# Seven block products in place of eight in a streaming-encoder block, with weight tiles of four k-tiles

## Chip, core and metric

The kernel runs on one NeuronCore of a Trainium2 chip. The metric is the device time of one execution in microseconds (us); less is better. The five engines have a queue of instructions each and wait for one another through semaphores: TensorE (PE in the rows; its weight loads are PEld), VectorE (DVE), ScalarE (ACT), GpSimd (POOL) and SyncE (SP), which issues the DMA loads here.

## What is computed

One layer in float32 on 256 tokens of width 2048:

```
h = x + 1/2 * swiglu(rms_norm(x), ffn1 weights)        # 2048 -> 5632 -> 2048
u = rms_norm(h); proj = u @ w_in; pooling branch and chunked attention branch
gates = sigmoid(u @ w_branch_gate + b)
h = h + (g_pool * (y_pool @ w_br_pool) + g_attn * (y_attn @ w_br_attn)) @ w_out
h = h + 1/2 * swiglu(rms_norm(h), ffn2 weights)
h = h + sigmoid(rms_norm(h) @ w_ple_gate) * (p @ w_ple)

def swiglu(x, w_gate, w_up, w_down):
    return (jax.nn.silu(x @ w_gate) * (x @ w_up)) @ w_down
```

All weights, some 400 MB, are read from HBM once.

## The kernel before

Every large product is made in three float32r matmuls: a float32 x is split into hi, a ScalarE cast to float32r, and lo = x - hi, a VectorE subtraction (`split`, L107 to L109), and a @ w becomes lo·hi + hi·hi + hi·lo, all into one accumulator (L153 to L155). Tokens lie in two tiles of 128 (`NT`), output columns in blocks of 512 (`NB`, a PSUM bank), K in tiles of 128.

`product` (L134) makes one block of 512 columns for both token tiles. A weight tile of two k-tiles (`KW`, 512 KB) is loaded into one of six buffers `wraw`, and split into `whi` and `wlo`, three buffers each (`weight`, L127). The split of the next tile is written ahead of this tile's 12 matmuls. The activation operand (`u`, or `hid` for the hidden columns) is split and turned to [k, token] once: a finished piece is transposed on TensorE some weight tiles later (`later`, `step`), so that TensorE does not wait for it.

A feed-forward network (`ffn`, L274) runs in three parts of 4, 4 and 3 blocks of hidden columns: for each block the gate product, then the up product, silu(gate) x up (`hb`, L290), and after a part the down products, added to `h` at L299. The 11 blocks of the two networks, the mixing stage between them and the last gate (`ple`, L542) all use `product`.

TensorE's instructions stand in the order written; those of the other engines are ordered by a scheduler once the first weight tiles are through (`ORDERED`). Buffers of a pool are taken in turn: the next tile of a name waits until the oldest one's last reader is done.

Of the kernel before, what the change touches and what calls it, by code (L numbers as in the profile page):

```python
# [16 lines left out]
P = 128  # L17
# [11 lines left out]
REACH = 16  # no window is longer  # L29
ORDERED = 5  # weight tiles until the scheduler orders the other engines  # L30
EPS = 1e-6
MASK_VALUE = -1e30
NB = 512  # output columns of one accumulator (a PSUM bank)
KB = 4  # k-tiles of one activation tile
KW = 2  # k-tiles of one weight tile
FFN_PARTS = (4, 4, 3)  # blocks of NB hidden columns between two down projections


@with_exitstack
def hybrid_block(ctx: ExitStack, tc: tile.TileContext, a: dict, out: bass.AP):  # L40
# [6 lines left out]
    ps_acc = ctx.enter_context(tc.tile_pool(name="ps_acc", bufs=5, space=bass.MemoryType.PSUM))  # L47
    ps_tp = ctx.enter_context(tc.tile_pool(name="ps_tp", bufs=3, space=bass.MemoryType.PSUM))
# [9 lines left out]
    # Vectors that are needed with their channel on the partitions: rows of 128, turned at once.  # L58
# [22 lines left out]
    def col(name, i=0, n=1):  # L81
        return cols[name][:, i:i + n]

# [1 line left out]
    # TensorE takes its instructions in the order written here. What turns a product's result is  # L85
    # written some weight tiles later, so that it never waits for the engines before it.
    waiting = []
    steps = [0]
    order = ExitStack()  # of the first weight tiles, where the loads of x and theirs take turns
# [16 lines left out]
    # hi keeps 12 significant bits, lo = x - hi the other 12: x == hi + lo.  # L106
# [4 lines left out]
    newest = [None]  # the weights' last load  # L111

    def load(w, kt, n0):
        raw = wpool.tile([P, KW, NB], F32, tag="wraw", name="wraw", bufs=6)
        newest[0] = nc.sync.dma_start(
            raw, w[kt * P:(kt + KW) * P, n0:n0 + NB].rearrange("(k p) n -> p k n", p=P)
        )
# [7 lines left out]
    loaded = []  # of the first product: loads that run between those of x  # L125

    def weight(w, kt, n0):  # L127
        raw = loaded.pop(0) if loaded else load(w, kt, n0)
        hi = wpool.tile([P, KW, NB], F32R, tag="whi", name="whi", bufs=3)
        lo = wpool.tile([P, KW, NB], F32R, tag="wlo", name="wlo", bufs=3)  # L130
        split(hi, lo, raw)
        return hi, lo

    def product(w, lhs, n0, k0=0):  # L134
        """[token, NB] accumulators of lhs @ w[k0*P:, n0:n0+NB]; lhs: Operands of up to KB k-tiles."""
        acc = [ps_acc.tile([P, NB], F32, tag="acc", name="acc") for _ in range(NT)]
        nk = sum(o.hi.shape[1] for o in lhs)
        ahead = weight(w, k0, n0)
        for kt in range(0, nk, KW):
            step()  # L140
            whi, wlo = ahead
            if kt + KW < nk:
                ahead = weight(w, k0 + kt + KW, n0)
            for o in {lhs[(kt + k) // KB] for k in range(KW)}:
                while o.missing:
                    step()
            for t in range(NT):
                tt = slice(t * P, (t + 1) * P)
                for k in range(KW):
                    o, kk = lhs[(kt + k) // KB], (kt + k) % KB  # L150
                    xh, xl = o.hi[:, kk, tt], o.lo[:, kk, tt]
                    first, last = kt + k == 0, kt + k == nk - 1
                    nc.tensor.matmul(acc[t], xl, whi[:, k, :], start=first, stop=False)  # L153
                    nc.tensor.matmul(acc[t], xh, whi[:, k, :], start=False, stop=False)  # L154
                    nc.tensor.matmul(acc[t], xh, wlo[:, k, :], start=False, stop=last)  # L155
        return acc

    class Operand:
        def __init__(self, pool, tag, bufs, nk=KB, missing=NT):
            self.hi = pool.tile([P, nk, SEQ], F32R, tag=tag + "hi", name=tag + "hi", bufs=bufs)  # L160
            self.lo = pool.tile([P, nk, SEQ], F32R, tag=tag + "lo", name=tag + "lo", bufs=bufs)
            self.missing = missing

    def turn(dst, src, t):
        """Columns of src [token, NB] become the k-tiles of dst at tokens of tile t."""
        tp = ps_tp.tile([P, NB], F32, tag="tp", name="tp")
        for j in range(KB):
            nc.tensor.transpose(tp[:, j * P:(j + 1) * P], src[:, j * P:(j + 1) * P], ident)  # L168
        tpv = tp.rearrange("p (j s) -> p j s", j=KB)
        tt = slice(t * P, (t + 1) * P)  # L170
        split(dst.hi[:, :, tt], dst.lo[:, :, tt], tpv)
        dst.missing -= 1

    def turn_gain(dst, srcs, ts, gain):
        """The same for h * gain, at the tokens of several tiles."""
        gained = []
        for src in srcs:
            tp = ps_tp.tile([P, NB], F32, tag="tp", name="tp")
            for j in range(KB):
                nc.tensor.transpose(tp[:, j * P:(j + 1) * P], src[:, j * P:(j + 1) * P], ident)  # L180
            g = work.tile([P, KB, P], F32, tag="gained", name="gained", bufs=2)
            nc.vector.tensor_tensor(  # L182
                out=g, in0=tp.rearrange("p (j s) -> p j s", j=KB),
                in1=gain.unsqueeze(2).to_broadcast([P, KB, P]), op=ALU.mult,
            )
            gained.append(g)
        for t, g in zip(ts, gained):
            tt = slice(t * P, (t + 1) * P)
            split(dst.hi[:, :, tt], dst.lo[:, :, tt], g)
            dst.missing -= 1  # L190

# [1 line left out]
    def rsqrt_mean(ssq, n, count, name, bufs):  # L193
# [6 lines left out]
        # One step of Newton takes the table's error out.  # L200
# [7 lines left out]

    class Norm:
# [3 lines left out]
        def __init__(self, gain):  # L213
            self.gain = gain
            self.ssq = work.tile([P, NT, D // NB], F32, tag="ssq", name="ssq", bufs=2)
            self.u = []

        def open(self, b):
            self.u.append(Operand(act, "u", D // NB))

        def turn(self, b, ts):
# [390 lines left out]
```

## Time and profile before

| what | value |
|---|---|
| median of 3 runs | 2147.14 us (2147.13 to 2147.52) |
| span of the profiled execution | 2146.3 us |
| PE busy | 2136.9 us (100%) |
| DVE busy | 1149.8 us (54%) |
| ACT busy | 944.4 us (44%) |
| DMA | 407.46 MB, 190 GB/s on average |

The span goes from the first to the last instruction of the profiled execution; the median of the runs is 0.8 us longer. Busy shares are averages over the whole span. Matmuls are pipelined and their shown durations overlap, so their rate is read from the distance between starts. "idle ... <-X" says that the engine stood before an instruction, and what ended the wait.

### The profile page before, as it was taken

Reading aid. Unit: us, or ns where it says so; the run is one execution under the profiler, and the core shown is the slowest. Engines: PE = TensorE matmul, PEld = TensorE weight load, DVE = VectorE, ACT = ScalarE, POOL = GpSimd, SP = SyncE. Lnnn points to the kernel's source line nnn. Section 1 sums busy time; section 2 is a strip of 40 time slices with the busy share of each in tenths; the row PEclk is TensorE's granted clock in tenths of the full one; section 3 lists DMA queues with packets and bytes.
Section 4 is the critical chain, followed back from the end, with each engine's and each line's share of the span. In section 5 each row is a group of like instructions: output and inputs, shape, how many; then the busy total and the mean of one; then the engine's idle time right before and its main releaser. Section 6 shows DMA issues by size and latency. Waiting matters only on the chain.

```text
span 2146.3 us, 24771 instructions
## 1 busy us (share of the span) xinstructions
PE 2136.9 (100%) x9626; PEld 1767.2 (82%) x9626; DVE 1149.8 (54%) x1196; ACT 944.4 (44%) x1069; POOL 3.0 (0%) x22
## 2 busy tenths in 40 slices
PE   9999999999999999999999999999999999999999
PEld 7888888888888888888888888888888888888887
DVE  5555545555455666555555555554545545455654
ACT  5444344443444544544444445444344443444553
POOL 0000000000000000000000000000000000000000
PEclk9999999999999999999999999999999999999999
DMA  7665566655665556665666556665566655665564
GB/s 245 188 186 193 192 193 191 187 190 195 190 191 189 181 186 184 192 189 171 198 197 197 187 187 191 191 190 186 195 191 193 186 188 194 195 188 186 186 196 137
DMA packets 212457, 407.46 MB, mean 190 GB/s; under 512 B 12842, under 2 KB 15732, under 8 KB 212340
## 3 DMA queue, kind: packets, MB, share of 16 engines
q1 hardware_dynamic: 212340, 405.89, 59.7%
q8 instruction: 75, 1.23, 0.2%
q14 instruction: 42, 0.34, 0.0%
HBM read 403.74 MB, written 2.10 MB: 189 GB/s over the span
## 4 chain that ended last, share of the span: by engine, by line
PE 99%; DMA 0%; DVE 0%; SPq 0%; ACT 0%; issue 0%; DVEq 0%; ACTq 0%
PE acc L155 32%; PE acc L153 32%; PE acc L154 32%; PE tp L168 1%; PE tp L180 1%; PE tp L464 0%; DMA h<-in_x_dram 0%; PE tp L393 0%; PE tp L347 0%; PE tp L425 0%; PE tp L417 0%; PE tp L450 0%; PE tp L451 0%; PE tp L426 0%; DVE sg L553 0%; DVE h L554 0%
## 5 line engine op out<-in xcount | busy, mean ns | idle before, releaser
L109 DVE TENSOR_TENSOR wlo<-wraw,whi 128x1024 fp32r<-128x1024 f32 x756 | 926.0, 1225 | 925.1 <-ACT whi L108 921.2
L108 ACT CAST whi<-wraw 128x1024 fp32r<-128x1024 f32 x756 | 793.5, 1050 | 1140.6 <-PE acc L154 1119.6
L153 PE MATMUL acc<-whi,ulo 128*128 128x512 f32 x2048 | 806.9, 394 | 0.0
L155 PE MATMUL acc<-wlo,uhi 128*128 128x512 f32 x2048 | 798.7, 390 | 0.5 <-DVE wlo L109 0.5
L154 PE MATMUL acc<-whi,uhi 128*128 128x512 f32 x2048 | 797.8, 390 | 0.0
L155 PEld LDWEIGHTS acc<-wlo,uhi 128*128 128x128 f32 x2048 | 384.9, 188 | 82.5 <-DVE wlo L109 1.3
L154 PEld LDWEIGHTS acc<-whi,uhi 128*128 128x128 f32 x2048 | 385.3, 188 | 78.1
L153 PEld LDWEIGHTS acc<-whi,ulo 128*128 128x128 f32 x2048 | 385.2, 188 | 77.8 <-ACT whi L108 0.2
L153 PE MATMUL acc<-whi,hidlo 128*128 128x512 f32 x832 | 326.7, 393 | 0.0
L155 PE MATMUL acc<-wlo,hidhi 128*128 128x512 f32 x832 | 324.1, 390 | 0.0
L154 PE MATMUL acc<-whi,hidhi 128*128 128x512 f32 x832 | 323.8, 389 | 0.0
L155 PEld LDWEIGHTS acc<-wlo,hidhi 128*128 128x128 f32 x832 | 156.1, 188 | 32.8
L154 PEld LDWEIGHTS acc<-whi,hidhi 128*128 128x128 f32 x832 | 156.3, 188 | 31.7
L153 PEld LDWEIGHTS acc<-whi,hidlo 128*128 128x128 f32 x832 | 156.2, 188 | 31.4
L109 DVE TENSOR_TENSOR hidlo<-tp,hidhi 128x512 fp32r<-128x512 f32 x52 | 35.5, 684 | 0.0
L284 ACT ACTIVATE sg<-acc,nr 128x512 f32<-128x512 f32 x44 | 29.9, 683 | 10.8 <-PE acc L155 10.8
L299 DVE SCALAR_TENSOR_TENSOR h<-acc,h 128x512 f32<-128x512 f32 x48 | 33.0, 688 | 0.9
L182 DVE TENSOR_TENSOR gained<-tp,vcol 128x512 f32<-128x512 f32 x32 | 21.8, 690 | 20.7 <-PE tp L180 20.7
L290 DVE SCALAR_TENSOR_TENSOR hb<-acc,nr,sg 128x512 f32<-128x512 f32 x44 | 32.5, 748 | 0.4 <-PE acc L155 0.4
L108 ACT CAST hidhi<-tp 128x512 fp32r<-128x512 f32 x52 | 30.2, 580 | 0.0
L108 ACT CAST uhi<-gained 128x512 fp32r<-128x512 f32 x32 | 19.7, 619 | 17.0 <-DVE gained L182 17.0
L168 PEld LDWEIGHTS tp<-ident,hb 128*128 128x128 f32 x176 | 21.8, 139 | 5.7
(111 smaller groups left out, 617.1 us busy)
## 6 DMA issues: line engine op xcount, KB each, us to landing
wraw<-in_ffn_w_gate_dram SPq DMA_DIRECT2D x176, 512.0 KB, 3.5
wraw<-in_ffn_w_up_dram SPq DMA_DIRECT2D x176, 512.0 KB, 3.5
wraw<-in_ffn_w_down_dram SPq DMA_DIRECT2D x176, 512.0 KB, 3.5
wraw<-in_w_in_dram SPq DMA_DIRECT2D x64, 512.0 KB, 3.5
wraw<-in_w_branch_gate_dram SPq DMA_DIRECT2D x64, 512.0 KB, 3.6
wraw<-in_w_out_dram SPq DMA_DIRECT2D x32, 512.0 KB, 4.1
wraw<-in_w_ple_gate_dram SPq DMA_DIRECT2D x32, 512.0 KB, 4.1
wraw<-in_w_br_pool_dram SPq DMA_DIRECT2D x16, 512.0 KB, 4.2
```

What stands on the lines that cost most here:

```text
L108: nc.scalar.copy(out=hi, in_=src)
L109: nc.vector.tensor_tensor(out=lo, in0=src, in1=hi.bitcast(F32), op=ALU.subtract)
L153: nc.tensor.matmul(acc[t], xl, whi[:, k, :], start=first, stop=False)
L154: nc.tensor.matmul(acc[t], xh, whi[:, k, :], start=False, stop=False)
L155: nc.tensor.matmul(acc[t], xh, wlo[:, k, :], start=False, stop=last)
L168: nc.tensor.transpose(tp[:, j * P:(j + 1) * P], src[:, j * P:(j + 1) * P], ident)
L180: nc.tensor.transpose(tp[:, j * P:(j + 1) * P], src[:, j * P:(j + 1) * P], ident)
L182: nc.vector.tensor_tensor(out=g, in0=tp.rearrange("p (j s) -> p j s", j=KB), in1=gain.unsqueeze(2).to_broadcast([P, KB, P]), op=ALU.mult,)
L284: nc.scalar.activation(s, ga[t], AF.Silu, scale=norm.r[t])
L290: nc.vector.scalar_tensor_tensor(hb, ua[t], norm.r[t], sg[t], op0=ALU.mult, op1=ALU.mult)
L299: nc.vector.scalar_tensor_tensor(piece, da[t], 0.5, piece, op0=ALU.mult, op1=ALU.add)
```

## The change

For half of K (the first two groups of four k-tiles) of two column blocks, the 2 x 2 blocks of tokens and k-groups (A11, A12, A21, A22: token tile, k-group) meet 2 x 2 blocks of weights (b11, b12, b21, b22: k-group, column side) in seven products in place of eight (Strassen-Winograd). Each is 4 k-tiles x 3 matmuls on one accumulator. The other k-groups stay plain ("school"): 24 matmuls on two accumulators. `block` replaces a pair of `product` calls: gate and up of one hidden block, two column blocks of a down product, two of the last gate.

The four sums of weights are made in place on VectorE on the raw tiles (L320), then split: t1 = b11 - b12, t2 = b22 - t1, t3 = b22 + b12, t4 = b21 - t2. The four sums of activations (s1 to s4, `Pair.combine`) are made once for each operand. A product's result that goes to two outputs leaves PSUM in between (`leave`, ScalarE; `leave_sum`, VectorE).

Weight tiles become four k-tiles (1 MB): five buffers `wraw`, which now also hold the activation sums, and two buffers each of `whi` and `wlo`, in place of three of half the size. The mixing stage uses the same tiles with the plain product. Accumulators get 6 banks in place of 5, transposes 2 in place of 3. Small tiles share one pool of ten (`piece_tile`).

```diff
-KW = 2  # k-tiles of one weight tile
+KW = 2
...
-        raw = wpool.tile([P, KW, NB], F32, tag="wraw", name="wraw", bufs=6)
+        return wpool.tile([P, KB, NB], F32, tag="wraw", name=name, bufs=5)
...
-        hi = wpool.tile([P, KW, NB], F32R, tag="whi", name="whi", bufs=3)
-        lo = wpool.tile([P, KW, NB], F32R, tag="wlo", name="wlo", bufs=3)
-        split(hi, lo, raw)
+    def parts(raw, nk=KB, at_once=KB):
+        hi = wpool.tile([P, KB, NB], F32R, tag="whi", name="whi", bufs=2)
+        lo = wpool.tile([P, KB, NB], F32R, tag="wlo", name="wlo", bufs=2)
+        for k in range(0, nk, at_once):
+            ks = slice(k, k + min(at_once, nk))
+            split(hi[:, ks, :], lo[:, ks, :], raw[:, ks, :])
...
+    def run(items):
+
+        for p in items[0][0]:
+            p()
+        for i, (_, mm) in enumerate(items):
+            if i + 1 < len(items):
+                for p in items[i + 1][0]:
+                    p()
+            mm()
...
+        def combine(self):
+            a11, a21 = self.x[:, 0, :], self.x[:, 1, :]
+            s1, s2, s3, s4 = (self.y[:, i, :] for i in range(4))
+            nc.vector.tensor_tensor(s1, s1, a21, op=ALU.subtract)
+            nc.vector.tensor_tensor(s2, s1, a11, op=ALU.add)
+            nc.vector.tensor_tensor(s3, a21, a11, op=ALU.subtract)
+            nc.vector.tensor_tensor(s4, s4, s2, op=ALU.subtract)
+            split(self.sh, self.sl, self.y)
+            self.ready = True
...
+        def combine(dst, x0, x1, op):
+            def f():
+                nc.vector.tensor_tensor(get(dst), get(x0), get(x1), op=op)
+            return f
...
+                for k in range(KB):
+                    ks = slice(k * P, (k + 1) * P)
+                    three(
+                        bank, xh[:, ks], xl[:, ks], wh[:, k, :], wl[:, k, :],
+                        bank.name not in begun, last and k == KB - 1, **kw,
+                    )
...
+        p1 = ([loads, part("b11")], seven(B, "A11", "b11", then=leave("s1", B, 0)))
+        p2 = ([combine("b11", "b11", "b12", ALU.subtract), part("b21")],
+              seven(A, "A12", "b21"))
+        p5 = ([part("t1", "b11")], seven(E, "S1", "t1", then=leave("s5", E, 1)))
+        p6 = ([combine("b11", "b22", "b11", ALU.subtract),
+               combine("b12", "b22", "b12", ALU.add), part("t2", "b11")],
+              seven(B, "S2", "t2", then=leave("u2", B, 0)))
+        p3 = ([part("b22")], seven(E, "S4", "b22", last=not rest))
+        p7 = ([part("t3", "b12")], seven(B, "S3", "t3", then=leave_sum))
+        t4 = combine("b21", "b21", "b11", ALU.subtract)
...
+            items = [p1, p2, p5, p6, p3]
+            ahead = [rest_item(i, 1, i == nr - 1) for i in range(nr)]
+            if nr > 1:
+                items += [ahead[0], p7] + ahead[1:]
+            else:
+                items += [p7] + ahead
+            lastprep, lastmm = items[-1]
+            items[-1] = (lastprep, lambda: (lastmm(), end2()))
+            items.append(([t4, part("t4", "b21")], seven(B, "A22", "t4", last=not rest)))
+            items += [rest_item(i, 0, i == nr - 1) for i in range(nr)]
...
-                ga = product(gate, norm.u, b * NB)
...
-                ua = product(up, norm.u, b * NB)
...
+                    c = block(
+                        [(up, b * NB), (gate, b * NB)], norm.pair, norm.groups[2:], 0,
+                        Scale(), gates, school_first=begins and b == 0,
+                    )
...
-                da = product(down, hid, n * NB, k0=b0 * KB)
...
+                    c = block(
+                        [(down, (n + 1) * NB), (down, n * NB)], pair, hid[2:], b0 * KB,
+                        (0.5, 0.5), second, taken=taken,
+                    )
```

VectorE at the seam into the sixth gate/up block of the first network, before: each weight tile's subtraction follows the last, with the two `hb` steps of the block that ended between them.

```order
L109 TENSOR_TENSOR wlo_2708<-wraw_2705,whi_2707 128x1024
L109 TENSOR_TENSOR wlo_2714<-wraw_2711,whi_2713 128x1024
L290 SCALAR_TENSOR_TENSOR hb_2699<-acc_2551,nr_326,sg_2547 128x512
L290 SCALAR_TENSOR_TENSOR hb_2701<-acc_2552,nr_326,sg_2549 128x512
L109 TENSOR_TENSOR wlo_2739<-wraw_2736,whi_2738 128x1024
L109 TENSOR_TENSOR wlo_2764<-wraw_2761,whi_2763 128x1024
L109 TENSOR_TENSOR hidlo_2698<-tp_2729,hidhi_2697 128x4x128
L109 TENSOR_TENSOR wlo_2782<-wraw_2779,whi_2781 128x1024
```

The same engine and place in the changed kernel, at the start of that block. wraw_2193 is b11 (then t1, then t2), wraw_2195 is b12 (then t3), wraw_2197 is b21 (then t4), wraw_2199 is b22; L112 is the subtraction, L320 a sum.

```order
L112 TENSOR_TENSOR wlo_2202<-wraw_2193,whi_2201 128x2048
L320 TENSOR_TENSOR wraw_2193<-wraw_2193,wraw_2195 128x2048
L612 SCALAR_TENSOR_TENSOR hb_2184<-acca_1923,nr_348,s1_1956 128x512
L617 SCALAR_TENSOR_TENSOR hb_2187<-accb_1924,nr_348,sg_2109 128x512
L615 TENSOR_TENSOR hb_2184<-hb_2184,sg_2106 128x512
L112 TENSOR_TENSOR wlo_2207<-wraw_2197,whi_2206 128x2048
L112 TENSOR_TENSOR wlo_2225<-wraw_2193,whi_2224 128x2048
L112 TENSOR_TENSOR hidal_1916<-blocks_2233,hidah_1915 128x512
L320 TENSOR_TENSOR wraw_2193<-wraw_2199,wraw_2193 128x2048
L320 TENSOR_TENSOR wraw_2195<-wraw_2199,wraw_2195 128x2048
L112 TENSOR_TENSOR wlo_2252<-wraw_2193,whi_2251 128x2048
L112 TENSOR_TENSOR wlo_2276<-wraw_2199,whi_2275 128x2048
```

Three of the four sums now stand between the subtractions, the second and third between those of t1 and t2; the pieces are twice as wide. The whole changed program has 480 subtractions of 128x2048 for weights and 144 such sums.

ScalarE at the same place, before:

```order
L108 CAST whi_2707<-wraw_2705 128x1024
L108 CAST whi_2713<-wraw_2711 128x1024
L108 CAST whi_2738<-wraw_2736 128x1024
L108 CAST whi_2763<-wraw_2761 128x1024
L108 CAST hidhi_2697<-tp_2729 128x4x128
L108 CAST whi_2781<-wraw_2779 128x1024
```

and in the changed kernel, from the cast of b11 to that of b22:

```order
L111 CAST whi_2201<-wraw_2193 128x2048
L111 CAST whi_2206<-wraw_2197 128x2048
L111 CAST whi_2224<-wraw_2193 128x2048
L326 ACTIVATE s1_2222<-accb_2190,nr_348 128x512
L462 COPY blocks_2233<-tp_2228 128x512
L111 CAST hidah_1915<-blocks_2233 128x512
L462 COPY blocks_2233<-tp_2255 128x512
L111 CAST whi_2251<-wraw_2193 128x2048
L326 ACTIVATE s5_2273<-acce_2191,nr_348 128x512
L111 CAST whi_2275<-wraw_2199 128x2048
```

The casts of wraw_2193 come three times, each after VectorE's sum into it; results that leave PSUM (s1, s5) and the turned hidden piece stand between them.

## Rows read from the trace of the kernel before

**Rows 1.** The page, parts 1, 2 and 4: busy, clock in 40 slices, chain.

```profile
PE 2136.9 (100%) x9626; PEld 1767.2 (82%) x9626; DVE 1149.8 (54%) x1196; ACT 944.4 (44%) x1069; POOL 3.0 (0%) x22
...
PEclk9999999999999999999999999999999999999999
...
PE acc L155 32%; PE acc L153 32%; PE acc L154 32%; PE tp L168 1%; PE tp L180 1%; PE tp L464 0%; DMA h<-in_x_dram 0%; PE tp L393 0%; PE tp L347 0%; PE tp L425 0%; PE tp L417 0%; PE tp L450 0%; PE tp L451 0%; PE tp L426 0%; DVE sg L553 0%; DVE h L554 0%
```

**Rows 2.** Timeline of TensorE: start us, duration us; first and last of 57 matmuls.

```profile
69.64 0.39 PE L154 MATMUL acc<-whi,uhi 128*128 128x512 f32 x1
...
82.34 0.39 PE L153 MATMUL acc<-whi,ulo 128*128 128x512 f32 x1
```

**Rows 3.** Waits, whole kernel: us in total, times, longest us.

```profile
ACT whi L108 <- PE acc L154: 1119.6, 715, 2.2
...
DVE wlo L109 <- ACT whi L108: 921.2, 660, 2.9
```

**Rows 4.** Groups by shape, VectorE: xcount | busy us, mean ns | idle before.

```profile
L109 DVE TENSOR_TENSOR wlo<-wraw,whi 128x1024 fp32r<-128x1024 f32 x756 | 926.0, 1225 | 925.1 <-ACT whi L108 921.2
...
L299 DVE SCALAR_TENSOR_TENSOR h<-acc,h 128x512 f32<-128x512 f32 x48 | 33.0, 688 | 0.9
L290 DVE SCALAR_TENSOR_TENSOR hb<-acc,nr,sg 128x512 f32<-128x512 f32 x44 | 32.5, 748 | 0.4 <-PE acc L155 0.4
...
L109 DVE TENSOR_TENSOR ulo<-gained,uhi 128x512 fp32r<-128x512 f32 x32 | 21.7, 686 | 0.3
...
L554 DVE TENSOR_TENSOR h<-h,sg 128x512 f32<-128x512 f32 x8 | 5.3, 687 | 0.1
```

**Rows 5.** Groups by shape, ScalarE: the casts of two sizes.

```profile
L108 ACT CAST whi<-wraw 128x1024 fp32r<-128x1024 f32 x756 | 793.5, 1050 | 1140.6 <-PE acc L154 1119.6 <-issue 11.6 <-ACT g L494 5.0
...
L108 ACT CAST uhi<-gained 128x512 fp32r<-128x512 f32 x32 | 19.7, 619 | 17.0 <-DVE gained L182 17.0
```

**Rows 6.** Timelines of TensorE, ScalarE and VectorE: one refill of a weight buffer.

```profile
159.23 0.39 PE L154 MATMUL acc<-whi,uhi 128*128 128x512 f32 x1
...
159.66 1.05 ACT L108 CAST whi<-wraw 128x1024 fp32r<-128x1024 f32 x1 [1.67 <-PE acc L154]
...
160.74 1.22 DVE L109 TENSOR_TENSOR wlo<-wraw,whi 128x1024 fp32r<-128x1024 f32 x1 [1.49 <-ACT whi L108]
```

**Rows 7.** Timelines of VectorE and TensorE at the start: a late low half.

```profile
21.14 1.22 DVE L109 TENSOR_TENSOR wlo<-wraw,whi 128x1024 fp32r<-128x1024 f32 x1 [0.26 <-ACT whi L108]
...
21.50 0.39 PE L154 MATMUL acc<-whi,uhi 128*128 128x512 f32 x1
22.41 0.50 PE L155 MATMUL acc<-wlo,uhi 128*128 128x512 f32 x1 [0.53 <-DVE wlo L109]
```

**Rows 8.** Chain of waits: transposes at one place of two gate/up blocks.

```profile
65.04 0.44 PE tp L168 x4
...
109.49 0.44 PE tp L168 x4
```

**Rows 9.** Windows of 2 us: busy of each engine, PEclk, DMA share, GB/s.

```profile
6.00:8.00 2.00, 0.64 (x6) 0.54 (x4) 1.75 (x3) 1.59 (x3) 0.00 (x0) 0.92 1.01 364
8.00:10.00 2.00, 1.31 (x7) 0.94 (x7) 1.74 (x3) 0.46 (x1) 0.00 (x0) 0.50 0.92 291
...
22.00:24.00 2.00, 1.59 (x7) 1.33 (x8) 0.36 (x1) 1.94 (x7) 0.00 (x0) 1.00 0.28 43
```

**Rows 10.** Timeline of TensorE at the low clock.

```profile
10.84 0.63 PE L155 MATMUL acc<-wlo,uhi 128*128 128x512 f32 x1
11.26 0.63 PE L153 MATMUL acc<-whi,ulo 128*128 128x512 f32 x1
```

**Rows 11.** The page, parts 3 and 6: the load queue and its weight loads.

```profile
q1 hardware_dynamic: 212340, 405.89, 59.7%
...
wraw<-in_ffn_w_gate_dram SPq DMA_DIRECT2D x176, 512.0 KB, 3.5
```

More of the change, by code (lines that the diff above doesn't have):

```diff
@@ L82, in col, with piece_tile @@
         return cols[name][:, i:i + n]
+    def piece_tile(name):
+        return work.tile([P, NB], F32, tag="piece", name=name, bufs=10)
     waiting = []
@@ new lines, in three, with school @@
+    def three(acc, xh, xl, wh, wl, first, last, **kw):
+        nc.tensor.matmul(acc, xl, wh, start=first, stop=False, **kw)
+        nc.tensor.matmul(acc, xh, wh, start=False, stop=False, **kw)
+        nc.tensor.matmul(acc, xh, wl, start=False, stop=last, **kw)
+    def school(accs, o, w, first, last, **kw):
+        wh, wl = w
+        for k0 in range(0, o.nk, KW):
+            step()
+            while o.missing:
+                step()
+            for t in range(NT):
+                for k in range(k0, k0 + KW):
+                    xh, xl = o.get(k, t)
+                    three(
+                        accs[t], xh, xl, wh[:, k, :], wl[:, k, :],
+                        first and k == 0, last and k == o.nk - 1, **kw,
+                    )
@@ L134, in product, with prepare, matmuls @@
+    def run(items):
[6 more added lines that the diff above has]
+            mm()
     def product(w, lhs, n0, k0=0):
         acc = [ps_acc.tile([P, NB], F32, tag="acc", name="acc") for _ in range(NT)]
[L137 to L144, printed above, removed]
+        items = []
+        kt = k0
+        for i, o in enumerate(lhs):
+            got = {}
+            def prepare(kt=kt, o=o, got=got):
+                got["w"] = parts(load(w, kt, n0, o.nk), o.nk)
+            def matmuls(i=i, o=o, got=got):
+                school(acc, o, got["w"], i == 0, i == len(lhs) - 1)
+            items.append(([prepare], matmuls))
+            kt += o.nk
+        run(items)
+        return acc
@@ new lines, in hybrid_block, with __init__, get, take @@
+    class Operand:
+        def __init__(self, pool, tag, bufs, nk=KB, missing=NT, tiles=None):
+            self.nk, self.missing = nk, missing
+            if tiles is None:
+                tiles = [
+                    pool.tile([P, nk, SEQ], F32R, tag=tag + s, name=tag + s, bufs=bufs)
+                    for s in ("hi", "lo")
+                ]
+            self.hi, self.lo = tiles
+        def get(self, k, t):
+            tt = slice(t * P, (t + 1) * P)
+            return self.hi[:, k, tt], self.lo[:, k, tt]
+        def take(self, t, write):
+            g = piece_tile("gained")
+            write(g)
+            self.take_from(t, g)
+        def take_from(self, t, src):
+            tt = slice(t * P, (t + 1) * P)
+            split(self.hi[:, :, tt], self.lo[:, :, tt], src.rearrange("p (k s) -> p k s", k=KB))
+            self.missing -= 1
@@ L145, in product @@
                 while o.missing:
                     step()
[L147 to L190, printed above, removed]
+                for t in range(NT):
+                    for k in range(kk, kk + KW):
+                        xh, xl = o.get(k, t)
+                        three(
+                            accs[t], xh, xl, wh[:, k, :], wl[:, k, :],
+                            accs[t].name not in begun, last and k == o.nk - 1, **kw,
+                        )
+                        begun.add(accs[t].name)
@@ L207, in hybrid_block, with turned, turn @@
     h = [act.tile([P, D], F32, tag=f"h{t}", name=f"h{t}") for t in range(NT)]
+    def turned(src):
+        tp = ps_tp.tile([P, NB], F32, tag="tp", name="tp")
+        for j in range(KB):
+            nc.tensor.transpose(tp[:, j * P:(j + 1) * P], src[:, j * P:(j + 1) * P], ident)
+        return tp
+    def turn(dst, src, t):
+        tp = turned(src)
+        if isinstance(dst, Operand):
+            dst.take_from(t, tp)
+        else:
+            dst.take(t, lambda f: nc.scalar.copy(out=f, in_=tp))
@@ L252, in load_x @@
         first = turn_vectors(["ffn1_norm"], nc.sync.dma_start)
-        for b in range(D // NB):
+        for b in (2, 3, 0, 1):
             for t in range(NT):
```

431 lines of the change are left out of this document (334 added, 97 removed).

## The prediction

> **What bounds the kernel now.** I read the page first, then the chain of waits, then the waits in total, then single groups of instructions. TensorE is busy for the whole span at full clock in each of the 40 slices, and the chain that ended last is 32% on each of the three matmul lines L153 to L155 [rows 1]: the reader is to see that no load, cast or subtraction ends last anywhere that matters. A 512-column matmul follows another every 0.2267 us: 56 steps lie between 69.64 and 82.34 [rows 2]. The two engines that split the weights wait for TensorE: ScalarE's cast waits 1119.6 us in all for the last matmul that reads a buffer, and VectorE's subtraction 921.2 us for the cast [rows 3]. So matmuls taken out are worth 0.2267 us each, as long as the splits go on arriving in time. That is the question here.
>
> **What goes.** A block of two column blocks and half of K was 2 x 2 x 8 x 3 = 96 matmuls and is 7 x 4 x 3 = 84. There are 11 gate/up blocks and 6 down blocks in each of the two networks and 2 blocks in the last gate, 36 in all: 432 matmuls, 432 x 0.2267 = 97.9 us, or 2.72 us for each block. Nothing else on TensorE's list changes in number.
>
> **Durations that the trace doesn't have.** Weights are now split in pieces of 128x2048. The cast takes 0.619 us at 512 and 1.050 at 1024 elements [rows 5], 0.431 for each 512 more, so 1.91 at 2048 (no less than 1.05, if size cost nothing, no more than 2.10, twice the row). The subtraction takes 0.686 and 1.225 us [rows 4], so 2.30 (1.23 to 2.45). The 144 sums of two raw weight tiles are f32 in and out; the all-f32 sum of 512 elements, L554, takes 0.687 us [rows 4], the same as a subtraction, so 2.30 as well (1.23 to 4 x 0.687 = 2.75). I take the straight line through two rows of the same instruction each time. VectorE's small steps stay at 0.69 to 0.75 us [rows 4].
>
> **The refill of a weight buffer.** This is where the change costs. Today there are three buffers of two k-tiles, each read by 12 matmuls. The cast starts 0.43 us after the start of the last matmul that reads the high half (159.23 to 159.66), the subtraction 0.03 after the cast's end (160.74) [rows 6], and TensorE goes on 0.05 us after the subtraction (22.36 to 22.41) [rows 7]. A refill takes 0.43 + 1.05 + 0.03 + 1.23 + 0.05 = 2.79 us; until the low half is needed TensorE has 0.45 (rest of the old triple) + 2 x 2.72 (two buffers) + 0.45 (two matmuls on the high half) = 6.35. The slack is 3.6 us. Where a low half does come late, at the start, rows 7 show what happens: the two matmuls on the high half run, and the third stands until 22.41.
>
> Afterwards there are two buffers of four k-tiles, and one of the seven products reads its buffer with 12 matmuls. A refill takes 0.43 + 1.91 + 0.03 + 2.30 + 0.05 = 4.72 us, and behind such a product the cover is 0.45 + 2.72 + 0.45 = 3.63: 1.09 us are missing. Behind a plain group (24 matmuls, 5.44 us) the cover is 6.35 and nothing is missing. Three plain groups of a block follow a product of 12 (after b22, t3 and t4): 3 x 1.09 = 3.3 us.
>
> **VectorE's queue in a steady block.** In the order VectorE has b11, sum, three steps of the block before, b21, t1, hidal, two sums, t2, b22. Set 0 where the block before starts its last plain group on TensorE. Cast b11 0.00 to 1.91; its subtraction to 4.24; b11 - b12 to 6.57. The three steps need TensorE's end of the old block at 5.44; they run to 8.45. Only then comes b21's subtraction, to 10.75. TensorE runs product b11 from 5.44 to 8.16, transposes (0.44 us [rows 8]), the two high matmuls of b21 to 9.05, and stands until 10.80: 1.75 us. It ends b21 at 13.07 and, past the second transposes, t1 at 16.2. VectorE meanwhile: t1's subtraction to 13.05, hidal to 13.7, b22 - b11 to 15.95, then b22 + b12 to 18.2. ScalarE can cast t2 from 15.98 to 17.89, so TensorE stands 1.7 us; t2's subtraction stands behind the second sum and ends at 20.45, and after two matmuls TensorE stands again for 2.1. Product b22 is in time.
>
> Together 1.75 + 1.7 + 2.1 + 3.3 = 8.8 us in a block where 2.72 are saved. A gate/up block takes 44.45 us now (65.04 to 109.49 [rows 8]) and should take 180 x 0.2267 + 0.9 (transposes) + 8.8 = 50.5. The eight weight loads of 1 MB are not the limit: the queue moves 405.89 MB in 59.7% of 2146.3 us of its engines [rows 11], 317 GB/s when busy, so 3.3 us for a load and 27 of the 50 us.
>
> **The sum.** 36 blocks x 8.8 = 317. In the second block of each of the 6 parts, the sums of the hidden operand are put ahead of a plain group (three at 0.69, a cast of 1.91, a subtraction of 2.30): 6 x 6.3 = 38. In the 12 down blocks eight additions of 0.69 stand in place of five steps, 1.8 us more in a queue that is full: 22. At the second network and at the last gate the normed operand's sums precede the third product: 2 x 7 = 14. The start, with its first weight tile four k-tiles deep: 10 (0 to 20). The clock, below: 24. That is 425 added and 98 taken, +327 on the profiled span of 2146.3, 2473; the median of the runs is 0.8 us above that span, so 2474. I say 2475.
>
> **The clock's part.** In the head of the trace TensorE is busy 0.64 of 2.00 us at clock 0.92, then 1.31 of 2.00 at 0.50, and it is back at 1.00 later, though TensorE works only 1.59 of 2.00 us between 22 and 24 [rows 9]; at 0.50, the 1.2 GHz level, matmuls start 0.42 us apart [rows 10]. In t2 the new queue leaves two matmuls in about 4.2 us. I count a fall in one of three blocks, at 2 us each: 12 x 2 = 24 (0 if it never falls, which leaves 2450).
> The Trainium skill, "TensorE: Matmul & The Clock Gate", section "HAM oscillation — how this bites in real kernels", says that waits between bursts of matmuls make the clock fall back, and that the next burst then starts slow. By that rule, taken strictly, every block pays, and the time is that of the third rival; without it the sum is 2450. The rows at the head agree that it falls after a thin stretch, and the one between 22 and 24 that not every wait brings it down.
>
> **Rivals.**
> First, the other side: the refill is hidden and the 2.72 us per block are gained. Its place is the handover from the subtraction to each product's third matmul; it holds if a piece of 2048 costs like one of 1024 (2.79 us of refill against 3.63 of cover, sums of 1.23). Stalls go, and 2146.3 - 97.9 + 10 + 0.8 = 2059. It decides where a block's stalls fall below 2.72 us. Against it: both instructions grow by 0.43 and 0.54 us per 512 elements [rows 4, 5]. 6%.
> The Trainium skill, "Trainium Kernel Development and Optimization", section "Best Practices", says to double-buffer for performance. By that rule two buffers would be enough and the time would be this rival's 2059; no row has a pool of two weight buffers, and the refill worked out above is longer than one product, so I give the rule no more than this chance.
> Second: VectorE does the sums earlier, in the plain groups, where it has time. Then only the three refills stay: 36 x 3.3 + 14 + 10 - 98 + 0.8 gives 2193. Against it: the second sum writes into the tile that t1's subtraction reads, so it cannot come before, and the low half of t1 has no buffer until product b11 is done. 10%.
> Third: the clock is at 0.50 in the five products of every block. 60 matmuls x 0.2 us = 12 us, of which the 5.5 us of stalls there are no longer seen: +6.5 x 36 = 234, so 2450 + 234 = 2684; in half the blocks, 2567. 12%.
> Fourth: loads. A block holds four of the five buffers of raw weights until its sums are done, and SP's queue, in which a load stands until VectorE lets its buffer go, issues in order. If the first split of a block came a load's length late each time, 36 x 3.3 = 119 and 2593. For it: one buffer ahead in place of today's six small ones; against it: 27 of 50 us, and the refill's stalls leave the loads more time. 8%.
>
> **How the numbers follow.** The forecast has 64%, its own range 2400 to 2550 (a block's stalls of 7 to 10.5 us). With the loads' case and half of the clock's inside, 2380 to 2600 holds 8 in 10. About 0.2% can be told from no change here. Faster by more than that: only the first rival, 6%; within it, a chance meeting of stalls and saving, 1%; slower 93%.
>
> **What would show it.** Right: TensorE busy near 85%, waiting on the third matmul's line for VectorE's low half; 128x2048 groups near 1.91 and 2.30 us; transposes of one place in two gate/up blocks about 50 us apart; VectorE at some 75% of the span (624 x 2.30 = 1435 us and about 400 of small steps). Wrong: the blocks 42 us apart with TensorE full (the first rival); stalls on ScalarE's cast released by a DMA (the fourth); a clock of 0.5 over whole slices (the third). The forecast fails as a whole if the stalls of a block are below 2.72 us.

## The result and the profile after

The changed kernel takes 2562.23 us (median of 4 runs, 2561.40 to 2562.68), the kernel before in the same session 2147.33: 1.193 times as long (95% interval 1.191 to 1.195). The forecast was 2475 with an own range of 2400 to 2550, the range as a whole 2380 to 2600: the direction and the main mechanism were right, the size 87 us short. First the page, parts 1, 2 and 4; it answers to [rows 1].

```profile
span 2560.9 us, 22679 instructions
PE 2228.7 (87%) x9194; PEld 1737.3 (68%) x9194; DVE 1767.9 (69%) x1237; ACT 1184.8 (46%) x1038; POOL 3.0 (0%) x22
...
PEclk8989899999998999999999999999998999999999
...
PE 33%; DVE 18%; ACT 6%; issue 3%; DMA 0%; DVEq 0%; ACTq 0%
DVE wlo L112 11%; ACT whi L111 5%; PE acc L142 5%; PE acc L141 5%; PE acc L140 5%; DVE wraw L320 5%; PE accb L142 2%; PE accb L140 2%; PE accb L141 2%; PE acce L142 2%; PE accd L141 1%; PE accd L140 1%; PE accd L142 1%; PE acce L140 1%; PE acce L141 1%
```

TensorE has 432 instructions fewer and stands for 332 us; VectorE's low halves and raw sums are now on the chain of waits, which was matmuls from end to end. Both stand next to each other in the waits of the whole kernel, where before TensorE waited 0.5 us in all for a low half and the long waits were those of ScalarE and VectorE [rows 3]:

```profile
engine line waited for: us in total, times, longest us
...
PE acca L142 <- DVE wlo L112: 77.7, 71, 3.2
PE acce L142 <- DVE wlo L112: 73.2, 74, 2.0
PE accb L142 <- DVE wlo L112: 62.4, 41, 2.0
PE accb L140 <- ACT whi L111: 50.1, 34, 3.8
PE acce L140 <- ACT whi L111: 21.6, 6, 5.3
PE accb L140 <- ACT s L326: 12.3, 2, 7.4
...
PE acc L140 <- ACT whi L111: 4.5, 2, 2.6
PE acc L142 <- DVE wlo L112: 4.2, 4, 1.6
```

L142 is the third matmul of a triple, the one on the low half; L140 is the first, on the high half. 71 + 74 + 41 = 186 waits of L142 are close to 5 x 36: three refills, b21 and t2 in each of the 36 blocks. acc is the accumulator of the plain products outside the blocks, in the mixing stage above all. No wait on a load stands near these. The durations that were read off a straight line, in groups by shape (after "|": busy us, mean ns, then the idle time before them), which answer to [rows 4, 5]:

```profile
L112 DVE TENSOR_TENSOR wlo<-wraw,whi 128x2048 fp32r<-128x2048 f32 x480 | 1094.6, 2289 | 618.2 <-ACT whi L111 617.8
L111 ACT CAST whi<-wraw 128x2048 fp32r<-128x2048 f32 x480 | 912.4, 1905 | 984.5 <-PE accb L141 430.0 <-PE accd L141 202.8 <-PE acc L141 195.6
L320 DVE TENSOR_TENSOR wraw<-wraw 128x2048 f32<-128x2048 f32 x144 | 327.3, 2287 | 1.7
```

One block, from TensorE's timeline (start, duration, in brackets the idle time before); these are all waits of one gate/up block, from the middle of its plain groups to the same place of the next block, and the matmuls after the longest:

```profile
395.77 0.50 PE L142 MATMUL acca<-wlo,uhi 128*128 128x512 f32 x1 [1.11 <-DVE wlo L112]
...
409.49 0.63 PE L453 MATMUL tp<-ident,hb 128*128 128x128 f32 x4 [0.28 <-DVE hb L615]
...
410.19 0.40 PE L141 MATMUL acca<-whi,uah 128*128 128x512 f32 x1
411.60 0.50 PE L142 MATMUL acca<-wlo,uah 128*128 128x512 f32 x1 [1.02 <-DVE wlo L112]
...
418.54 0.50 PE L140 MATMUL accb<-whi,usl 128*128 128x512 f32 x1 [1.19 <-ACT whi L111]
418.87 0.40 PE L141 MATMUL accb<-whi,ush 128*128 128x512 f32 x1
421.01 0.50 PE L142 MATMUL accb<-wlo,ush 128*128 128x512 f32 x1 [1.74 <-DVE wlo L112]
421.34 0.40 PE L140 MATMUL accb<-whi,usl 128*128 128x512 f32 x1
421.58 0.58 PE L141 MATMUL accb<-whi,ush 128*128 128x512 f32 x1
421.96 0.63 PE L142 MATMUL accb<-wlo,ush 128*128 128x512 f32 x1
422.38 0.63 PE L140 MATMUL accb<-whi,usl 128*128 128x512 f32 x1
...
424.52 0.63 PE L142 MATMUL accb<-wlo,ush 128*128 128x512 f32 x1
424.94 0.43 PE L140 MATMUL acce<-whi,usl 128*128 128x512 f32 x1
...
429.04 0.50 PE L142 MATMUL acce<-wlo,uhi 128*128 128x512 f32 x1 [0.68 <-DVE wlo L112]
...
438.47 0.50 PE L142 MATMUL acce<-wlo,uhi 128*128 128x512 f32 x1 [0.93 <-DVE wlo L112]
...
448.03 0.50 PE L142 MATMUL acca<-wlo,uhi 128*128 128x512 f32 x1 [1.11 <-DVE wlo L112]
```

Read it in starts, since durations overlap. The block lasts 448.03 - 395.77 = 52.26 us, against 44.45 before [rows 8] and 50.5 forecast. acca at 411.60 is product b21, accb at 418.54 and 421.01 is t2; 429.04, 438.47 and 448.03 are the three refills. VectorE explains t2 (its timeline over the same stretch):

```profile
409.26 4.49 DVE L112 TENSOR_TENSOR wlo<-wraw,whi 128x2048 fp32r<-128x2048 f32 x2
413.66 0.69 DVE L112 TENSOR_TENSOR hidal<-blocks,hidah 128x512 fp32r<-128x512 f32 x1
414.26 4.49 DVE L320 TENSOR_TENSOR wraw<-wraw 128x2048 f32<-128x2048 f32 x2
418.67 4.52 DVE L112 TENSOR_TENSOR wlo<-wraw,whi 128x2048 fp32r<-128x2048 f32 x2
```

Two low halves, a small one, two raw sums, and only then t2's low half: VectorE goes from one to the next without a gap, and TensorE takes t2's high half at 418.54 and stands for the low one until 421.01. The clock falls behind that wait. Windows of 2 us (busy of PE, PEld, DVE, ACT, POOL, then PEclk, DMA share, GB/s):

```profile
419.00:421.00 2.00, 0.27 (x2) 0.00 (x0) 2.00 (x2) 1.86 (x2) 0.00 (x0) 1.00 0.00 0
421.00:423.00 2.00, 1.99 (x6) 1.62 (x7) 2.00 (x1) 0.00 (x0) 0.00 (x0) 0.66 0.00 0
423.00:425.00 2.00, 2.00 (x7) 1.51 (x6) 2.00 (x2) 0.24 (x1) 0.00 (x0) 0.50 0.24 47
425.00:427.00 2.00, 2.00 (x10) 1.65 (x9) 0.69 (x2) 2.00 (x2) 0.00 (x0) 0.99 0.96 353
```

TensorE is busy 0.27 of 2.00 us, then runs at 0.50 (1.2 GHz), with starts 0.43 us apart in place of 0.23, and after 424.94 it is back at full clock (0.99 from 425 to 427).

### The profile page after: what moved, and what is told of

It is laid out like the page before. It is cut to its first block, busy times and chain, and to the rows that moved or that the text cites. A ratio compares the mean times of both kernels' runs of the same rounds, so it can differ in the third digit from the quotient of the medians.

```text
span 2560.9 us, 22679 instructions
## 1 busy us (share of the span) xinstructions
PE 2228.7 (87%) x9194; PEld 1737.3 (68%) x9194; DVE 1767.9 (69%) x1237; ACT 1184.8 (46%) x1038; POOL 3.0 (0%) x22
## 3 DMA queue, kind: packets, MB, share of 16 engines
q8 instruction: 72, 1.18, 0.2%
## 4 chain that ended last, share of the span: by engine, by line
PE 33%; DVE 18%; ACT 6%; issue 3%; DMA 0%; DVEq 0%; ACTq 0%
DVE wlo L112 11%; ACT whi L111 5%; PE acc L142 5%; PE acc L141 5%; PE acc L140 5%; DVE wraw L320 5%; PE accb L142 2%; PE accb L140 2%; PE accb L141 2%; PE acce L142 2%; PE accd L141 1%; PE accd L140 1%; PE accd L142 1%; PE acce L140 1%; PE acce L141 1%
## 5 line engine op out<-in xcount | busy, mean ns | idle before, releaser
L112 DVE TENSOR_TENSOR wlo<-wraw,whi 128x2048 fp32r<-128x2048 f32 (+1 forms) x492 | 1108.9, 2263 | 634.2 <-ACT whi L111 633.8
L111 ACT CAST whi<-wraw 128x2048 fp32r<-128x2048 f32 (+1 forms) x492 | 924.5, 1884 | 1000.2 <-PE accb L141 440.6
L320 DVE TENSOR_TENSOR wraw<-wraw 128x2048 f32<-128x2048 f32 x144 | 327.3, 2287 | 1.7
L142 PE MATMUL accb<-wlo,ush 128*128 128x512 f32 x192 | 94.6, 493 | 38.6 <-DVE wlo L112 38.6
L140 PE MATMUL accb<-whi,usl 128*128 128x512 f32 x192 | 91.1, 475 | 39.8 <-ACT whi L111 27.5
L142 PE MATMUL acce<-wlo,uhi 128*128 128x512 f32 x184 | 81.0, 440 | 43.2 <-DVE wlo L112 43.2
L140 PE MATMUL acc<-whi,ual 128*128 128x512 f32 x256 | 103.8, 405 | 4.5 <-ACT whi L111 4.5
L142 PE MATMUL acc<-wlo,uah 128*128 128x512 f32 x256 | 101.7, 397 | 2.7 <-DVE wlo L112 2.7
L140 PE MATMUL acc<-whi,ulo 128*128 128x512 f32 x256 | 101.9, 398 | 0.0
L141 PE MATMUL acc<-whi,uah 128*128 128x512 f32 x256 | 101.2, 395 | 0.0
L142 PE MATMUL acca<-wlo,uhi 128*128 128x512 f32 x192 | 77.5, 404 | 27.0 <-DVE wlo L112 27.0
L142 PE MATMUL acc<-wlo,uhi 128*128 128x512 f32 x256 | 100.0, 390 | 0.0
L141 PE MATMUL acc<-whi,uhi 128*128 128x512 f32 x256 | 99.8, 390 | 0.0
L140 PE MATMUL acce<-whi,ulo 128*128 128x512 f32 x184 | 76.5, 416 | 21.6 <-ACT whi L111 21.6
L142 PEld LDWEIGHTS accb<-wlo,ush 128*128 128x128 f32 x192 | 45.3, 236 | 58.5 <-DVE wlo L112 48.6
L142 PE MATMUL acce<-wlo,ush 128*128 128x512 f32 x192 | 77.2, 402 | 7.9 <-DVE wlo L112 7.9
L142 PEld LDWEIGHTS acce<-wlo,uhi 128*128 128x128 f32 x184 | 36.5, 198 | 70.0 <-DVE wlo L112 63.6
L140 PEld LDWEIGHTS accb<-whi,usl 128*128 128x128 f32 x192 | 44.4, 231 | 58.2 <-ACT whi L111 36.8
L140 PE MATMUL acce<-whi,usl 128*128 128x512 f32 x192 | 79.5, 414 | 0.0
L140 PE MATMUL accd<-whi,ulo 128*128 128x512 f32 x192 | 78.0, 406 | 0.0
L142 PE MATMUL accd<-wlo,uhi 128*128 128x512 f32 x192 | 77.5, 404 | 0.0
```

The source lines that it names most:

```text
L111: nc.scalar.copy(out=hi, in_=src)
L112: nc.vector.tensor_tensor(out=lo, in0=src, in1=hi.bitcast(F32), op=ALU.subtract)
L140: nc.tensor.matmul(acc, xl, wh, start=first, stop=False, **kw)
L141: nc.tensor.matmul(acc, xh, wh, start=False, stop=False, **kw)
L142: nc.tensor.matmul(acc, xh, wl, start=False, stop=last, **kw)
L320: nc.vector.tensor_tensor(get(dst), get(x0), get(x1), op=op)
```

## The experiments

All were timed beside the kernel before (2147.7 to 2148.3 us), and ratios are to it. The quoted text of each says what was expected of it.

**1. High halves first.** The two matmuls of each triple that read the high half are written for all four k-tiles (and both token tiles of a plain group) before the ones on the low half; the same matmuls, in another order.

```
-    three(bank, xh[:, ks], xl[:, ks], wh[:, k, :], wl[:, k, :], ...)
+    high(bank, xh[:, ks], xl[:, ks], wh[:, k, :], ...)
+for k in range(KB):
+    low(bank, xh[:, ks], wl[:, k, :], last and k == KB - 1, **kw)
```

> Each product and plain group runs all its matmuls on the high half first, then those on the low half; engines and amounts of work stay. Refill theory: behind a product of 12 the cover of a refill becomes 0.23 + 4 x 0.23 + 2.72 + 8 x 0.23 = 5.7 us against 4.7, so the three stalls of about 1.1 us go in each of 36 blocks, about 0.8 us of the wait in b21's product, and some 1.4 us of the second wait in t2's: 36 x 5.5 = 198 less, and the clock falls less, 2310 to 2360 us. Loads theory (the five raw buffers come free too late): nothing changes for the loads, 2540 to 2570. Theory that VectorE's sheer amount of work is the bound: 2520 to 2570.

Measured 2343.49 us, ratio 1.091 (1.089 to 1.092): 219 us of the 415 go by order alone. VectorE has the same work (its 480 low halves take 1092.6 us, 1094.6 in the changed kernel), so the time was lost in when a low half is needed, not in how much VectorE does. What is left in TensorE's waits:

```profile
PE accb L145 <- ACT whi L111: 97.4, 35, 4.2
PE acce L145 <- ACT whi L111: 22.9, 7, 3.8
...
PE acca L149 <- DVE wlo L112: 14.2, 33, 3.7
```

Here L145 is the first matmul and L149 the one on the low half. The waits on low halves have all but gone; 35 waits for t2's high half remain, one in each block but one, since ScalarE cannot cast t2 before VectorE has added it up.

**2. No sums.** The four sums of raw weight tiles in each block are left out (the products then read the tiles as loaded, so the output is not the layer's).

```
-    nc.vector.tensor_tensor(get(dst), get(x0), get(x1), op=op)
+    for n in (dst, x0, x1):
+        get(n)
```

> The four sums of weight tiles are left out (the seven products run on the unsummed tiles, so seven splits stay). Queue theory: VectorE has 9.2 us less in each block; both waits around t2 and the fall of the clock behind them go, and a refill's 1.1 us stays behind each product of 12: stalls of about 5 us a block in place of about 11, 2290 to 2350 us. Refill theory alone, without the queue: the three stalls and no more were there, so 2540 to 2562. If VectorE's work is the bound: 36 x 9.2 = 330 less, 2230.

Measured 2342.11 us, ratio 1.090 (1.089 to 1.092): 220 us go, in the queue theory's range and not the 330 that VectorE's lesser work would give. The refills stay, as they should when only the queue is relieved:

```profile
PE acce L142 <- DVE wlo L112: 66.4, 92, 2.0
PE acca L142 <- DVE wlo L112: 54.6, 69, 1.6
PE accb L142 <- DVE wlo L112: 23.0, 39, 2.0
```

accb's waits on the low half fall from 62.4 to 23.0, and its 50.1 us for the cast to 0.2; the granted clock rises from 0.946 to 0.985.

**3. Something to do in t2's waits.** Five matmuls that nobody reads are put ahead of t2 and seven between its second and third matmul, so that TensorE works through both waits.

```
+if name == "t2":
+    idle(5)
 for k in range(KB):
     (high half's two matmuls)
+    if name == "t2" and k == 0:
+        idle(7)
     (low half's matmul)
```

> Twelve matmuls of 512 columns whose result nobody reads stand in the two waits of t2's product (five ahead of it, seven before its first matmul on the low half), about as long as the waits. Clock theory: the waits stay and the granted clock no longer falls behind t2 (eight matmuls at 0.43 in place of 0.23 us in each block now): 36 x 1.6 = 58 less, about 2505 us, granted clock 0.98. If the fall is hidden by VectorE's queue anyway: 2555 to 2570. If matmuls in a wait delay those behind them: 2580 or more.

Measured 2529.93 us, ratio 1.178 (1.176 to 1.180): 32 us less than the changed kernel, for 432 matmuls more, and between the branches expected (about 2505, and 2555 or more). The rows of one block show that the clock does not fall in it:

```profile
409.76 1.79 PE L359 MATMUL idle<-uah 128*128 128x512 f32 x7
411.64 0.50 PE L373 MATMUL accb<-wlo,ush 128*128 128x512 f32 x1
411.98 0.40 PE L367 MATMUL accb<-whi,usl 128*128 128x512 f32 x1
...
412.68 0.39 PE L367 MATMUL accb<-whi,usl 128*128 128x512 f32 x1
```

Counted over the whole trace, matmuls that start 0.40 to 0.46 us after the one before without a wait are 429 in the changed kernel (85.6 us more than at 0.2267 us each) and 171 here, the fillers counted with the others (34.3 us): 51.3 us of low clock go, and the granted clock is 0.976 in place of 0.946. Not all of it is seen in the time, because the filling is not free: 12 x 36 x 0.2267 = 98 us of it stand where TensorE's waits on accb (62.4 on the low half, 50.1 on the cast) fall to 10.8 and 18.4 while the other three large sums (acca and acce on the low half, acce on the cast) grow by 14: 69 us of waits gone. 98 - 69 - 51 = -22, where 32 were measured; the other 10 are not accounted for. A filler cures most of the clock's falls and pays more than half of what that gives back in filling.

**4. Tiles of four k-tiles alone.** The block products and the sums are undone; two buffers of four k-tiles and pieces of 128x2048 stay, with eight plain products of 24 matmuls a weight tile.

```
-def block(sides, pair, rest, k0, scales, done2, ...):   # seven products
+def both(w, n0, lhs, k0, turn_first):                   # plain triples, one tile after another
```

> One part of the change alone: weight tiles of four k-tiles, two buffers of each half, five of raw weights; every block made of eight plain products (24 matmuls on a buffer), no sums. Refill theory: the cover behind 24 matmuls is 6.4 us against 4.7, so there is next to no stall: 2147 to 2185 us. Loads theory: 1 MB tiles in five buffers come late here as well: 2250 or more.

Measured 2193.65 us, ratio 1.021 (1.020 to 1.023). TensorE is busy 2161.1 us, 99% of the span: behind 24 matmuls the refill is covered, as the arithmetic of the prediction has it, and loads of 1 MB into five buffers cost 46 us at the most. The result is 9 us above the range expected. The head shows a part of the 46 us: 38.81 busy us of the first 50 against 45.67 before. The plain products at the seams of the mixing stage and in the last gate show another: there TensorE waits 4.5 us for casts and 7.7 us for low halves, where the kernel before has 0.5. The rest was not located.

**5. Both.** High halves first and no sums (again not the layer's output).

```
(the edits of 1 and 2)
```

> Both at once: high halves first, and the four sums of weight tiles left out (the output is not the layer's). If refills and VectorE's queue are two causes that add up, next to nothing waits in the blocks and the 98 us of left-out matmuls show against the plain tiles' 2194: 2100 to 2150 us, clock 0.99. If both edits had removed the same waits, it stays near either: 2290 to 2340. If the loads' buffers were a cause of their own, 2200 to 2290.

Measured 2135.48 us, ratio 0.994 (0.993 to 0.996). The two causes very nearly add up: 219 from order, 220 from sums, 427 together. It also prices the scheme: with both stalls away the seven products are 12 us faster than the kernel before, 39 short of the 2193.65 - 97.9 = 2096 that the missing matmuls alone would give on the tiles of experiment 4.

**6. Two of the four sums on GpSimd.** Experiment 1, with the sums for t3 and t4 moved from VectorE.

```
+POOLED = ('b12', 'b21')
-nc.vector.tensor_tensor(get(dst), get(x0), get(x1), op=op)
+e = nc.gpsimd if dst in POOLED else nc.vector
+e.tensor_tensor(get(dst), get(x0), get(x1), op=op)
```

> High halves first, and the sums for t3 and t4 on GpSimd in place of VectorE; nothing is left out. Queue theory: t2's subtraction no longer stands behind a sum that it does not need, and VectorE has 4.6 us less in a block: 2343 less 36 x 2 to 2.6, so 2240 to 2275 us, as long as a GpSimd sum of 128x2048 takes less than about 6 us. If VectorE and GpSimd hold each other up while both read and write SBUF, VectorE's 128x2048 rows grow beyond 2.29 us and it gains little: 2300 to 2400.

Measured 2471.55 us, ratio 1.151 (1.149 to 1.153): 128 us slower than experiment 1, a miss beyond both branches. The timelines show an instruction of VectorE that lasts until GpSimd's sum is over (GpSimd, then VectorE):

```profile
394.69 4.59 POOL L329 TENSOR_TENSOR wraw<-wraw 128x2048 f32<-128x2048 f32 x1 [34.52 <-DVE wraw L329]
```

```profile
394.39 0.74 DVE L621 SCALAR_TENSOR_TENSOR hb<-acca,nr,s 128x512 f32<-128x512 f32 x1
395.16 0.75 DVE L626 SCALAR_TENSOR_TENSOR hb<-accb,nr,sg 128x512 f32<-128x512 f32 x1
395.83 4.00 DVE L624 TENSOR_TENSOR hb<-hb,sg 128x512 f32<-128x512 f32 x1
```

While GpSimd's sum runs, from 394.69 to 399.28, VectorE's product of an accumulator (L626) takes its usual 0.75 us, but the one of two SBUF tiles (L624) 4.00 in place of 0.68: it ends 0.55 us after GpSimd. Over the kernel 72 sums leave VectorE (328.8 - 168.8 = 160 us) and its busy time rises by 66, from 1766.9 to 1833.3. TensorE's waits grow with it: on accb's low half from 5.5 us in experiment 1 to 81.0, and for the hidden piece that L624 makes from 3.7 to 44.4. The Trainium skill, "SBUF — State Buffer", section "SBUF: two separate sides", says that VectorE and GpSimd share a pair of ports under an exclusive lock, which an instruction of VectorE with two SBUF inputs needs against a GpSimd one that reads SBUF; these rows agree (4.00 us with two SBUF tiles, 0.75 with an accumulator).

**7. Reordered, in smaller pieces, with GpSimd.** Experiment 6, with the order of products b11, t1, b21, b22, t2, and every weight tile split in two pieces of 128x1024.

```
-items = [p1, p2, p5, p6, p3]
+items = [p1, p5, p2, p3, p6]
-def parts(raw, nk=KB, at_once=KB):
+def parts(raw, nk=KB, at_once=KW):
```

> High halves first; products in the order b11, t1, b21, b22, t2, so that the sum for t2 has two products to be made in; splits in pieces of 128x1024; the sums for t3 and t4 on GpSimd. Queue theory: the waits around t2 and b21 shrink below 1 us a block and the 2.72 us saved begin to show; what is left is the start, the hidden operand's sums and the wait for a result that leaves its accumulator: 2150 to 2200 us. If GpSimd holds VectorE up: 2250 or more.

Measured 2470.79 us, ratio 1.151 (1.149 to 1.153), in the branch in which GpSimd holds VectorE up. GpSimd's sums take 5.84 us in the mean here and VectorE's pieces 1.376 (1.219 where GpSimd has no sums, experiment 10).

**8. Smaller pieces alone.** The changed kernel, with splits of 128x1024 (a buffer is still four k-tiles).

```
-def parts(raw, nk=KB, at_once=KB):
+def parts(raw, nk=KB, at_once=KW):
```

> Every weight tile of four k-tiles is split in two pieces of two k-tiles (cast and subtraction 128x1024 in place of 128x2048); the changed kernel is otherwise kept. By the kernel before a piece costs 1.05 us of cast and 1.22 us of subtraction, so the first low half stands 2.7 us after a buffer comes free and no longer 4.7 us, under the 3.6 us that a product of 12 gives it. Refill theory: the 1.09 us missing three times in each of the 36 blocks go, 118 us, and the waits in front of the two products with sums before them shrink by the shorter subtraction, at most 1.1 us each, 80 us: 2360 to 2450 us. If it is VectorE's amount of work, not the first piece's delay, nothing is gained, since the pieces add some 0.15 us each pair: 2560 to 2620.

Measured 2387.39 us, ratio 1.111 (1.110 to 1.113): 175 us go, inside the refill theory's range, though VectorE works more (1800.8 us busy, 1767.9 in the changed kernel). The waits on the low half shrink, from 62.4 us for accb, 73.2 for acce and 77.7 for acca, to this:

```profile
PE accb L142 <- DVE wlo L112: 46.5, 37, 1.6
...
PE acce L142 <- DVE wlo L112: 14.3, 12, 1.4
...
PE acca L142 <- DVE wlo L112: 7.8, 9, 2.3
```

So it was the delay of the first piece that stalled the refill. accb's waits for the cast do not shrink: 74.2 us, 50.1 in the changed kernel.

**9. Both of 1 and 8.**

```
(the edits of 1 and 8)
```

> The high halves first, and the splits in pieces of two k-tiles. If the first run's 219 us already hold all that a refill can give, only the sums queued on VectorE are left and the pieces change nothing but their own overhead: 2340 to 2370 us. If the waits that are left in it (ACT's cast released late, 97 us in front of accb) still hold part of the refill, the first piece's earlier end takes up to 0.9 us of each of some 37 to 74 waits: 2280 to 2320.

Measured 2315.41 us, ratio 1.078 (1.077 to 1.080): 28 us below experiment 1, within what was expected if the cast's late release still held part of the refill. The 97.4 us in front of accb become 83.5.

**10. Reordered, sums on VectorE.** Experiment 7 without GpSimd.

```
-POOLED = ('b12', 'b21')
+POOLED = ()
```

> The seventh run with its sums back on VectorE: high halves first, products in the order b11, t1, b21, b22, t2, splits in pieces of two k-tiles, no sum on GpSimd. If GpSimd's sums cost more than they took off VectorE (its 72 sums of 4.8 to 5.8 us, beside which VectorE's 128x512 sum took 4.00 us in place of 0.68), this is faster than the seventh run's 2471 by at least 100 us: 2250 to 2350 us. If the new order was what made the seventh run slow, it stays at 2430 to 2500.

Measured 2302.80 us, ratio 1.072 (1.071 to 1.074): 168 us below experiment 7, inside the range expected, so GpSimd was the cause there and not the order. The order itself is worth 13 us over experiment 9. This is the best version that computes the whole layer, and it stays 155 us behind the kernel before: its waits for t2's cast, which follows VectorE's sum, are still 72.0 us, and its clock is 0.968. A third buffer of four k-tiles was not tried.

## Why the prediction was right, and where its size was off

**Direction and mechanism: right.** The profiled span grew by 2560.9 - 2146.3 = 414.6 us where the prediction had 425 - 98 = 327. Its rule, that stalls of a block exceed the 2.72 us saved, is borne out by TensorE's waits and by experiments 1, 2 and 5, which take the stalls away in two halves and end 12 us below the time before.

**Durations: right.** 1.905 us for the cast (1.91 forecast), 2.289 for the subtraction and 2.287 for the sum (2.30). Of the signs, TensorE is busy 87% (85 given), VectorE 69% (75 given).

**Refill: right.** Lost starts beyond 0.2267 us at 429.04, 438.47 and 448.03 are 0.83, 1.09 and 1.26, together 3.18; forecast 3 x 1.09 = 3.27. Experiment 4 shows next to none behind 24 matmuls in the two networks, experiment 8 that a first piece of half the length takes most of it away.

**VectorE's queue: right in place, slightly long.** b21 lost 1.18 us (1.75 forecast), t2's first matmul 1.35 (1.7), its third 1.91 (2.1). With the refills that is 7.62 us in this block, where 8.8 were forecast.

**The clock: right in kind, too small.** This is the step that failed in size: "a fall in one of three blocks, at 2 us each", 24 us. The place was right, t2, and so was the size of one fall: in the block shown some 8 matmuls run 0.2 us late, 1.6 us. What failed is how often. The clock fell behind t2 in 33 of the 36 blocks, not in 12: 281 slow matmuls, 56.1 us. The other slow matmuls lie mostly where the sum had no fall: behind the hidden operand's sums in the third block of each part, in the down blocks, at the head and in the mixing stage. Together they are 429 matmuls and 85.6 us, against 21 and 4.1 us in the kernel before, so 81.5 us where 24 stood. The rows at the head of the trace before could not tell how often it would fall, and the middle was chosen.

The Trainium skill, "TensorE: Matmul & The Clock Gate", section "HAM oscillation — how this bites in real kernels", says that the clock falls back in the waits between bursts of matmuls. This trace agrees in those 33 blocks. In the other three the waits are the same and the clock stays up: at 529.95 us t2's first matmul has waited 1.23 us and its third, at 532.37, 1.68, and the granted clock from 533 to 535 is 1.00. What sets those three apart no run here shows. The third rival was wrong on how long a fall lasts: about 8 matmuls and not 60. Its time for half the blocks, 2567, is 5 us from the measured one by chance.

**The rest: 30 us short.** Without the clock, 414.6 + 97.9 - 81.5 = 431 us of stalls and surcharges stand where the prediction had 401. So 57 of the 87 us were the clock and 30 these. Counted start by start over both traces, the stalls are not what was short: in front of matmuls that waited more than 0.15 us, 370 us more are lost than before. The other 61 us are starts that come a little late without a wait, which the sum had at nothing. After a wait, for instance, the next start comes some 0.1 us late (411.60 to 411.94 in place of 411.83), six times a block, 22 us in 36 blocks. The block shown does not bring the 30 us: less the clock's 1.6 us it lasts 50.7, and 50.5 were forecast. One place that the sum left out is the mixing stage, where the plain products (acc) now wait 8.7 us and waited 0.5 before.

**Two terms of the sum.** The hidden operand's sums stand in the third block of a part, not in the second; their size is about right (t2 comes 59.14 us after that of the block before, where the step before is 52.27, so 6.9 us with the clock, and 6.3 were forecast). The 14 us for the second network and the last gate were luck. They were given for the normed operand's sums ahead of the third product; TensorE in fact waits 12.3 us ahead of t2 for an accumulator. The result that has to leave it is scaled by the new norm's factor `nr`, which VectorE finishes only then, its small steps standing between the sums and subtractions of 2.3 us (ScalarE, then TensorE):

```profile
1531.78 0.69 ACT L326 ACTIVATE s<-accb,nr 128x512 f32<-128x512 f32 x1 [3.17 <-DVE nr L445]
```

```profile
1532.52 0.80 PE L140 MATMUL accb<-whi,usl 128*128 128x512 f32 x1 [7.40 <-ACT s L326]
```

**Rivals.** Refill hidden (2059): refuted. The Trainium skill, "Trainium Kernel Development and Optimization", section "Best Practices", says to double-buffer so that DMA and compute overlap; that two buffers are enough is the prediction's reading of it. Two were enough in experiment 4, where each is read by 24 matmuls, and were not where one is read by 12. Sums early (2193; its terms add up to 2192): refuted by the timeline of VectorE above. Loads (2593): close to the time measured but wrong in cause; TensorE's and ScalarE's large waits name no load, and experiments 1, 2 and 8 speed the kernel up by 175 to 220 us with the same loads. In the block shown, the loads all but stand still from 405 to 423 us (8 GB/s at most in a window of 2 us) and then run at 353 GB/s, without TensorE waiting for them.

## What to carry to other kernels

Fewer matmuls are worth their time only while every operand that another engine prepares arrives within the shorter cover that is left: work out the refill (release, cast, subtraction, handover) against the matmuls that read the other buffer, and the longest run of the vector queue in front of each product, before counting the saving. Where an operand comes in two halves, let TensorE use up all of the first before it asks for the second; here that was worth 219 us and costs nothing. And where a steady loop has a wait with almost nothing in it, count a fall of the clock for every turn of the loop: here it came in 33 turns of 36.

## What was not expected of the hardware

A GpSimd sum of two 128x2048 f32 tiles took 4.59 us and held VectorE's 128x512 sum of two SBUF tiles up from 0.68 to 4.00 us, while an instruction of VectorE on an accumulator beside it kept its 0.75 us. Moving 160 us of sums to an idle engine made the kernel 128 us slower, and 168 in the reordered version. The clock fell behind the same wait in 33 blocks and not in three.

Matmuls that nobody reads kept the clock up (171 slow matmuls in place of 429), yet won only 32 us, since they fill more time than the waits had.
